# Convolution taps as one chain per channel group, the second half's first groups during the first attention, and squares summed on GpSimd

## The chip, the core and the metric

The kernel runs on one core of a Trainium2 chip. The metric is device time in microseconds (us) of one execution, lower is better; the kernel before takes 1140.39 us, the median of 3 runs. A core has five engines with their own instruction queues: TensorE (PE, matrix products), VectorE (DVE), ScalarE (ACT), GpSimd (POOL) and SyncE (SP, which only issues transfers here). Each engine works through its own queue strictly in order and waits for semaphores of the others. Products land in PSUM, which has eight banks of 128 x 512 float32; GpSimd does not touch PSUM in this kernel. Everything else lies in SBUF.

## The reference

One decoder layer over 1024 tokens of 1024 channels, in float32: an input projection, whose columns feed windowed attention (8 heads of 64, 2 key heads, window 128) and a convolution group (512 channels, 31 taps), both RMS-normalised and projected together, then a gated feed-forward layer with a 3-tap convolution. Both sub-layers end in a LayerNorm of the scaled input plus their output.

```python
def conformer_conv_group(a, gate, dw_w, dw_b, ln_g, ln_b):
    h = a * jax.nn.sigmoid(gate)
    h = causal_depthwise_conv(h, dw_w, dw_b)        # 31 taps, per channel
    h = layer_norm(h, ln_g, ln_b)                   # over the 512 channels
    return jax.nn.silu(h)

# sliding_window_gqa: each block of 128 queries sees its own and the previous key block
scores = jnp.where(mask, scores + bias[:, :, None], -jnp.inf)
m = jnp.maximum(jnp.max(scores, axis=-1, keepdims=True), sink)
p = jnp.exp(scores - m)
denom = jnp.sum(p, axis=-1, keepdims=True) + jnp.exp(sink - m)
probs = (p / denom).astype(v.dtype)

# hybrid_mixer
q, k, v, a, gate = jnp.split(x @ w_in + b_in, [Q_END, K_END, V_END, A_END], axis=-1)
y = jnp.concatenate([rms_norm(y_attn, attn_out_gain), rms_norm(y_conv, conv_out_gain)], axis=-1)
mix = y @ w_out + b_out
x = layer_norm(DEEPNORM_ALPHA * x + mix, ln1_g, ln1_b)

# conv_ffn
h = causal_depthwise_conv(x @ w_up, dw_w, dw_b)     # 3 taps
g, u = jnp.split(h, 2, axis=-1)
ffn = (jax.nn.silu(g) * u) @ w_down
x = layer_norm(DEEPNORM_ALPHA * x + ffn, ln2_g, ln2_b)
```

## The kernel before

The tokens are worked in two halves of 512 (`H` = 0 and 1), each as four tiles of 128. Channels lie on the 128 partitions, so one channel group is a tile of 128 x 512, and the convolution has four groups per half. For accuracy each float32 operand of a large product is split into a high and a low part (`wh`, `wl`; line 231 on ACT, line 233 on POOL), and three products replace one (`mm3`, lines 265, 266, 268).

Each step of a half is a Python generator: loading x (`x`), the gated input of the convolution (`0` for the first half, `g` for the second; `glu`), key and value (`j`, `k`), queries (`i`, `q`), convolution (`c`, `C`), its norm (`n`, `N`), attention (`a`, `A`), output projection (`o`, `O`), first LayerNorm (`l`, `L`) and the first six column pairs of the feed-forward layer for the first half (`f`). The string `SCRIPT` sets the program order: each letter runs its generator by one step, and `c` and `C` run to their end at once. From that program order a scheduler, with its own estimate of durations, sets the final order on every engine when the kernel is built. After the script the other sixteen column pairs are worked for both halves together (`joint`), then the rest of the second half.

**The convolution** (`conv_pair`, lines 405 to 430). The taps of one channel group are summed in one PSUM bank: line 421 starts the sum on DVE, and each further tap, line 425, reads the bank, adds one shifted, scaled copy of the input `hconv`, and writes it back. The oldest `KOFF` taps (4 in the first half, 5 in the second) are scaled on ACT (line 411) and summed on POOL (line 415), and line 430 adds the two sums. Two groups are worked together, tap by tap in turn, in the two banks tagged `C`. A dependency keeps all taps in one order.

**Its norm** (`conv_norm`, lines 441 to 485) sums the four groups over the channels: POOL adds (443, 444), one product with ones (445), DVE subtracts the mean (449), ACT squares (451), and sixteen products of one column (456, four token tiles by four groups) give the variance. Lines 462 and 464 spread the inverse deviation over the partitions, 469 to 472 apply it with swish and gain, 475 squares again, and sixteen more products (480) give the mean square for the RMS norm.

**The attention** (`attn`) has sixteen units per half: four token tiles, two key heads, two pairs of query heads. A unit's front makes scores (511), adds the bias and takes the row extreme on DVE (516), and the exponential on ACT (521) with the sink's exponential per head (523). After the second unit of a key head the denominator is made on DVE (527, 528) and ACT scales the four probability tiles (531). One unit later the tiles are transposed on PE (541) and split (543 on ACT, 544 on DVE), and one unit after that they are multiplied with the values (562 to 564). At the end of a token tile the result is scaled and split (569, 571), squared (574), and after three more units summed by four products of one column (581).

The output projection of a half (642 to 648, added up in 652 and 654) needs the whole norm of the convolution and the attention of the token tile. Line 627 prepares its accumulators. Other lines named below: 278, 281 and 282 transpose and split; 311 to 313 are the LayerNorm; 677 to 698 and 724 the first half's feed-forward work; 751 sums that prepare the joint stage; 806 and 808 its three-tap convolution.

## Time and profile before

| | |
|---|---|
| median of 3 runs | 1140.39 us (1139.77 to 1141.25) |
| the profiled execution | 1140.95 us, of which the profiled span is 1139.2 us |
| mean granted TensorE clock | 0.967 |
| PE busy | 1084.8 us (95%) |
| DVE busy | 776.6 us (68%) |
| POOL busy | 599.1 us (53%) |
| ACT busy | 521.3 us (46%) |
| HBM traffic | 84 MB, 74 GB/s |

The engines' shares are means over stages with different limits, so the stages are read one by one, in windows of the trace. The table of windows has, for each stretch of the span, the busy microseconds of each engine with its instruction count, then the granted clock and the share of the transfer engines. A matmul's record counts as busy also while the clock is lowered, so a busy PE may still be a slow one. A row of a group gives line, engine, operation, tiles and shape, then busy time, the mean duration of one, and the idle time ahead of them with what ended it.

### The profile page before, as it was taken

How to read it: one execution, taken by the hardware profiler on the slowest of the kernel's cores; microseconds unless marked ns; L12 is line 12 of the kernel's file. 1: busy time of each engine (PE TensorE's matmuls, PEld its weight loads, DVE VectorE, ACT ScalarE, POOL GpSimd, SP SyncE). 2: the span in 40 equal slices, each digit the busy share in tenths (PEclk: the TensorE clock that was granted, in tenths of full speed). 3: DMA queues.
4: the chain of work that ended last, by engine and by line, in shares of the span. 5: the costliest groups of instructions: out<-in, count | busy, mean ns of one | idle time of the engine just before them, and what ended most of it. 6: DMA issues, size and time to landing. Idle time of an engine off the chain costs nothing.

```text
span 1139.2 us, 14637 instructions
## 1 busy us (share of the span) xinstructions
PE 1084.8 (95%) x5257; PEld 903.9 (79%) x5257; DVE 776.6 (68%) x1414; ACT 521.3 (46%) x1031; POOL 599.1 (53%) x468
## 2 busy tenths in 40 slices
PE   7999999998888999989999999999999999999997
PEld 5877788888876899867778787878878787888875
DVE  3699555999996355998565747474656656559656
ACT  4536897673659432444424334251524242442530
POOL 4739645446461165834837465564636373835561
PEclk9999988999968899999999999999999999999998
DMA  5534212233220034113211112121212021223421
GB/s 179 167 97 116 72 32 66 83 93 119 67 93 19 1 121 120 57 38 92 73 38 56 56 38 75 37 75 37 65 28 75 19 75 37 70 99 115 125 93 74
DMA packets 115642, 85.21 MB, mean 75 GB/s; under 512 B 20354, under 2 KB 108017, under 8 KB 115569
## 3 DMA queue, kind: packets, MB, share of 16 engines
q1 hardware_dynamic: 112368, 78.92, 23.2%
q10 hardware_dynamic: 3201, 5.35, 1.3%
q8 instruction: 41, 0.67, 0.2%
q14 instruction: 32, 0.26, 0.1%
HBM read 80.05 MB, written 4.21 MB: 74 GB/s over the span
## 4 chain that ended last, share of the span: by engine, by line
PE 45%; DVE 5%; ACT 1%; DMA 0%; POOL 0%; issue 0%; POOLq 0%; ACTq 0%
PE psC L800 2%; PE psC L798 2%; PE psC L797 2%; PE psS L800 2%; PE psS L797 2%; PE psS L798 2%; PE psA L800 2%; PE psA L798 2%; PE psA L797 2%; PE psS L717 2%; PE psS L718 2%; PE psS L719 2%; PE psA L717 1%; PE psC L717 1%; PE psA L718 1%; PE psA L719 1%
## 5 line engine op out<-in xcount | busy, mean ns | idle before, releaser
L233 POOL TENSOR_TENSOR wl<-raw,wh 128x512 fp32r<-128x512 f32 x196 | 263.0, 1354 | 223.4 <-PE psA L268 86.3
L231 ACT CAST wh<-raw 128x512 fp32r<-128x512 f32 x196 | 118.7, 619 | 172.0 <-PE psA L266 19.2
L233 POOL TENSOR_TENSOR wl<-ts,wh 128x512 fp32r<-128x512 f32 x64 | 82.5, 1296 | 149.6 <-ACT wh L231 136.5
L265 PE MATMUL psA<-x,wh 128*128 128x512 f32 x336 | 138.2, 411 | 7.9 <-DVE z L682 3.5
L266 PE MATMUL psA<-x,wh 128*128 128x512 f32 x336 | 137.4, 409 | 0.0
L425 DVE SCALAR_TENSOR_TENSOR psC<-hconv,const,psC 128x512 f32<-128x512 f32 x196 | 135.8, 742 | 0.0
L231 ACT CAST wh<-ts 128x512 fp32r<-128x512 f32 x64 | 39.4, 622 | 174.4 <-PE psS L719 31.0
L268 PE MATMUL psA<-x,wl 128*128 128x512 f32 x336 | 90.6, 404 | 0.6 <-POOL wl L233 0.6
L265 PEld LDWEIGHTS psA<-x,wh 128*128 128x128 f32 x336 | 66.1, 197 | 24.0 <-issue 4.4
L266 PEld LDWEIGHTS psA<-x,wh 128*128 128x128 f32 x336 | 66.0, 197 | 14.6 <-issue 0.7
L268 PEld LDWEIGHTS psA<-x,wl 128*128 128x128 f32 x336 | 63.9, 193 | 15.8 <-issue 1.2
L293 POOL TENSOR_TENSOR tiny<-tiny,const 128x1 f32<-128x1 f32 (+1 forms) x28 | 27.6, 989 | 61.3 <-DVE tiny L292 61.3
L233 POOL TENSOR_TENSOR ol<-or,oh 128x512 fp32r<-128x512 f32 x32 | 41.0, 1307 | 26.8 <-PE psY L564 15.4
L724 DVE TENSOR_TENSOR acc<-psS,acc 128x512 f32<-128x512 f32 x52 | 35.6, 687 | 26.9 <-PE psS L719 26.9
L797 PE MATMUL psS<-x,wh 128*128 128x512 f32 x112 | 43.6, 389 | 0.0
L797 PE MATMUL psA<-x,wh 128*128 128x512 f32 x112 | 43.6, 389 | 0.0
L798 PE MATMUL psA<-x,wh 128*128 128x512 f32 x112 | 43.6, 389 | 0.0
L798 PE MATMUL psS<-x,wh 128*128 128x512 f32 x112 | 43.6, 389 | 0.0
L797 PE MATMUL psC<-x,wh 128*128 128x512 f32 x112 | 43.6, 389 | 0.0
L798 PE MATMUL psC<-x,wh 128*128 128x512 f32 x112 | 43.6, 389 | 0.0
L415 POOL TENSOR_TENSOR cp<-cp,cp 128x512 f32<-128x512 f32 x28 | 36.0, 1286 | 13.0 <-ACT cp L411 13.0
L836 POOL TENSOR_TENSOR ts<-raw,ts 128x512 f32<-128x512 f32 x32 | 41.6, 1299 | 1.2
(340 smaller groups left out, 3084.3 us busy)
## 6 DMA issues: line engine op xcount, KB each, us to landing
raw<-in_w_up SPq DMA_DIRECT2D x56, 512.0 KB
raw<-in_w_down SPq DMA_DIRECT2D x28, 512.0 KB
raw<-in_w_in SPq DMA_DIRECT2D x20, 512.0 KB
raw<-in_x SPq DMA_DIRECT2D x8, 512.0 KB
raw<-in_w_in SPq DMA_DIRECT2D x16, 256.0 KB
acc<-in_x SPq DMA_DIRECT2D x8, 512.0 KB
or<-in_w_out SPq DMA_DIRECT2D x64, 64.0 KB
or<-in_w_out SPq DMA_DIRECT2D x8, 512.0 KB
```

The source lines that it names most:

```text
L231: nc.scalar.copy(out=h, in_=part)
L233: nc.gpsimd.tensor_tensor(out=l, in0=part, in1=f(h), op=ALU.subtract)
L265: m.append(nc.tensor.matmul(out=o, lhsT=wh[kt], rhs=xh[kt], start=kt == 0, stop=False))
L266: m.append(nc.tensor.matmul(out=o, lhsT=wh[kt], rhs=xl[kt], start=False, stop=False))
L268: m.append(nc.tensor.matmul(out=o, lhsT=wl[kt], rhs=xh[kt], start=False, stop=kt == KT - 1))
L415: nc.gpsimd.tensor_tensor(out=extra[c], in0=extra[c], in1=prod, op=ALU.add)
L425: tap(nc.vector.scalar_tensor_tensor(out=to, in0=src, scalar=cdw(k, c), in1=chains[c], op0=ALU.mult, op1=ALU.add))
L717: m.append(nc.tensor.matmul(out=o, lhsT=gh[:, tsl], rhs=wh, start=j == 0, stop=False))
L797: m.append(nc.tensor.matmul(out=o, lhsT=wh[k], rhs=xh[k], start=k == 0, stop=False))
L798: m.append(nc.tensor.matmul(out=o, lhsT=wh[k], rhs=xl[k], start=False, stop=False))
L800: m.append(nc.tensor.matmul(out=o, lhsT=wl[k], rhs=xh[k], start=False, stop=k == 3))
L836: nc.gpsimd.tensor_tensor(out=t, in0=x0, in1=x1, op=ALU.subtract)
```

## The change

One change with seven pieces:

- **Script.** The second half's gated inputs begin earlier (two `g` stand ahead of the first convolution). `C` becomes a step per channel group: two groups are started right behind the first half's norm, ahead of most of the first attention, the third and fourth between later attention steps. The later letters move with them.
- **Chains.** `conv_group` works one channel group at a time in one bank `C`; the other bank becomes `N`, for the norm.
- **Token sums.** Both sums of squares of the norm are first added over the four groups on POOL (three additions of 128 x 512, line 433 of the changed kernel), so that four products of one column (435) replace sixteen.
- **Attention squares.** Two POOL additions (572, of 256 and 128 columns) let one product (578) replace four per token tile.
- **Sink.** One DVE addition (514) and one exponential of four columns (521) per key head replace four exponentials of one column.
- **Scaling.** The probability tiles are scaled by the inverse denominator on POOL (526), no longer on ACT.
- **Banks.** The joint stage and the second LayerNorm's transposes name the bank `N` in their rotations.

```diff
-SCRIPT = ('0hx00j0hxixxiiiacaaaaaaaaaaaaannnaaagaggqqgaaaqkqoAAAoAAAAAo'
-          'ACAoAAllAANAAAANAlAlfNfAOOOfsOsssffLLLLffff')
+SCRIPT = ('0hx00j0hxixxiiiggacaaaaaaaaaaaaannnCCaaagagCkCqqaaaqqoAAAoA'
+          'AAAAoAAoNAlAlNAlAlNAAAAfAfAAOOOfsOsssffLLLLffff')
...
-      'joint': 'ATSACSYC',
-      'tail': 'T', 'out0': 'A', 'out1': 'A', 'ln0': 'A', 'ln1': 'TC', 'sum1': 'T', 'up0': 'A', 'up1': 'AY', 'down0': 'SY', 'down1': 'S'}
-PS = {'A': 2, 'S': 2, 'T': 1, 'Y': 1, 'C': 2}
+      'joint': 'ATSACSYN',
+      'tail': 'T', 'out0': 'A', 'out1': 'A', 'ln0': 'A', 'ln1': 'TCN', 'sum1': 'T', 'up0': 'A', 'up1': 'AY', 'down0': 'SY', 'down1': 'S'}
+PS = {'A': 2, 'S': 2, 'T': 1, 'Y': 1, 'C': 1, 'N': 1}
...
-    def conv_pair(H, c0, dst):
...
-        chains = {c: psB(tag="C") for c in (c0, c0 + 1)}
         for k in range(KW - 1, KO - 1, -1):
-            for c in (c0, c0 + 1):
...
+    def conv_group(H, c, dst):
         KO = KOFF[H]
+        for k in range(KO):
+            slot = 2 * (c % 2) if k == 0 else 1
+            prod = at(64 * 4 * UNIT + 4 * (HC + slot * HALF), [P, HALF], F32, "cp")
+            nc.scalar.mul(out=prod, in_=hconv[H, c][:, k:k + HALF], mul=cdw(k, c))
+            if k == 0:
+                extra = prod
+            else:
+                nc.gpsimd.tensor_tensor(out=extra, in0=extra, in1=prod, op=ALU.add)
+        total = psB(tag="C")
+        for k in range(KW - 1, KO - 1, -1):
+            src = hconv[H, c][:, k:k + HALF]
+            if k == KW - 1:
+                tap(nc.vector.tensor_scalar(out=total, in0=src, scalar1=cdw(k, c), scalar2=cdb[c],
+                                            op0=ALU.mult, op1=ALU.add))
+            else:
+                tap(nc.vector.scalar_tensor_tensor(out=dst if k == KO else total, in0=src, scalar=cdw(k, c),
+                                                   in1=total, op0=ALU.mult, op1=ALU.add))
+        nc.gpsimd.tensor_tensor(out=dst, in0=dst, in1=extra, op=ALU.add)
...
+    def token_sums(o, sqs):
+        for a, b in ((0, 1), (2, 3), (0, 2)):
+            nc.gpsimd.tensor_tensor(out=sqs[a], in0=sqs[a], in1=sqs[b], op=ALU.add)
+        for t in range(TB):
+            nc.tensor.matmul(out=o[:, t:t + 1], lhsT=sqs[0][:, t * P:(t + 1) * P], rhs=ones[:, 0:1],
+                             start=True, stop=True)
...
-        for t in range(TB):
-            for c in range(4):
-                nc.tensor.matmul(out=var[:, t:t + 1], lhsT=sqs[c][:, t * P:(t + 1) * P], rhs=ones[:, 0:1],
-                                 start=c == 0, stop=c == 3)
+        token_sums(var, sqs)
...
+            if pr == 1:
+                nc.vector.tensor_tensor(out=es, in0=sink[:, g * 4:g * 4 + 4], in1=m, op=ALU.add)
             for i in range(2):
...
-                nc.scalar.activation(out=es[:, j:j + 1], in_=sink[:, h:h + 1], func=AF.Exp, bias=m[:, j:j + 1],
-                                     scale=1.0)
             pts[u] = pt
             if pr == 1:
+                nc.scalar.activation(out=es, in_=es, func=AF.Exp)
                 nc.vector.tensor_tensor(out=den, in0=den, in1=es, op=ALU.add)
                 nc.vector.reciprocal(out=den, in_=den)
                 for j in range(4):
                     q = pts[t, g, j // 2][:, j % 2, lo:]
-                    nc.scalar.mul(out=q, in_=q, mul=den[:, j:j + 1])
+                    nc.gpsimd.tensor_scalar(out=q, in0=q, scalar1=den[:, j:j + 1], scalar2=1.0,
+                                            op0=ALU.mult, op1=ALU.mult)
...
                 nc.scalar.square(out=sq, in_=yp[t])
+                for w in (2 * P, P):
+                    nc.gpsimd.tensor_tensor(out=sq[:, 0:w], in0=sq[:, 0:w], in1=sq[:, w:2 * w], op=ALU.add)
...
-            for i in range(4):
-                nc.tensor.matmul(out=ms[:, 0:1], lhsT=sqs[t][:, i * P:(i + 1) * P], rhs=ones[:, 0:1],
-                                 start=i == 0, stop=i == 3)
+            nc.tensor.matmul(out=ms[:, 0:1], lhsT=sqs[t][:, 0:P], rhs=ones[:, 0:1], start=True, stop=True)
...
     for k in SCRIPT:
-        if k in 'cC':
+        if k == 'c':
             drain(steps[k])
```

Three places of the new order follow. The first is DVE at the start of the first half's convolution (`hconv_30_238` is its input, `psC_...` a bank). Before:

```order
L358 SCALAR_TENSOR_TENSOR hconv_30_238<-psA_287,const_1_61,z_43_342 128x512
L421 TENSOR_SCALAR psC_799<-hconv_30_238,const_1_61 128x512
L425 SCALAR_TENSOR_TENSOR psC_798<-hconv_30_238,const_1_61,psC_798 128x512
L357 COPY hconv_71_1553<-hconv_30_238 128x30
L425 SCALAR_TENSOR_TENSOR psC_799<-hconv_30_238,const_1_61,psC_799 128x512
L425 SCALAR_TENSOR_TENSOR psC_798<-hconv_30_238,const_1_61,psC_798 128x512
L425 SCALAR_TENSOR_TENSOR psC_799<-hconv_30_238,const_1_61,psC_799 128x512
```

And in the changed kernel:

```order
L418 TENSOR_SCALAR psC_915<-hconv_30_238,const_1_61 128x512
L282 TENSOR_TENSOR x_39_263<-psS_272,x_38_262 128x4x128
L421 SCALAR_TENSOR_TENSOR psC_915<-hconv_30_238,const_1_61,psC_915 128x512 x12
L358 SCALAR_TENSOR_TENSOR hconv_30_238<-psA_287,const_1_61,z_43_342 128x512
L421 SCALAR_TENSOR_TENSOR psC_915<-hconv_30_238,const_1_61,psC_915 128x512
L357 COPY hconv_54_825<-hconv_30_238 128x30
L421 SCALAR_TENSOR_TENSOR psC_915<-hconv_30_238,const_1_61,psC_915 128x512 x11
```

Two banks that took turns have become one bank, where each tap reads what the tap just ahead of it wrote; the first chain starts with one gated group in place of two. The second place is DVE in the first attention, from the last tap of the first half on (`cy` is a finished convolution, `hank` the probability tiles, `ph` their transposes, `hconv_1553` or `hconv_825` the second half's input). Before:

```order
L425 SCALAR_TENSOR_TENSOR cy_780<-hconv_238,const_61,psC 128x512
L544 TENSOR_TENSOR ph_948<-psT,ph_948 128x256
L516 ISA hank_256,tiny_60<-psS,bias_573,const_61 128x256
L516 ISA tiny_60 128x1
...
L358 SCALAR_TENSOR_TENSOR hconv_1553<-psA,const_61,z_407 128x512
L544 TENSOR_TENSOR ph_967<-psT,ph_967 128x256
L527 TENSOR_TENSOR tiny_60<-tiny_60 128x4
L528 RECIPROCAL tiny_60<-tiny_60 128x4
```

And now:

```order
L418 TENSOR_SCALAR psC<-hconv_825,const_61 128x512
L540 TENSOR_TENSOR ph_1090<-psT,ph_1090 128x256
L510 ISA hank_256,tiny_60<-psS,bias_573,const_61 128x256
L510 ISA tiny_60 128x1
...
L421 SCALAR_TENSOR_TENSOR psC<-hconv_825,const_61,psC 128x512
L514 TENSOR_TENSOR tiny_60<-const_61,tiny_60 128x4
L421 SCALAR_TENSOR_TENSOR psC<-hconv_825,const_61,psC 128x512
L522 TENSOR_TENSOR tiny_60<-tiny_60 128x4
L421 SCALAR_TENSOR_TENSOR psC<-hconv_825,const_61,psC 128x512
L523 RECIPROCAL tiny_60<-tiny_60 128x4
```

Taps of the second half stand between the first attention's rows, and mostly alternate with them. The third place is POOL in the first attention, around the last additions of the first half's channel sum (`wl` is the low part of a weight tile, `cp` and `nsum` belong to the convolution, `nsq` are squares, `sq` the attention's). Before:

```order
L444 TENSOR_TENSOR nsum_1330<-nsum_1330,nsum_1331 128x512
L233 TENSOR_TENSOR wl_174<-raw_166,wh_284 128x512
L415 TENSOR_TENSOR cp_781<-cp_781,cp_783 128x512
L233 TENSOR_TENSOR wl_205<-raw_201,wh_168 128x512
L415 TENSOR_TENSOR cp_781<-cp_781,cp_783 128x512
L415 TENSOR_TENSOR cp_790<-cp_790,cp_783 128x512
L233 TENSOR_TENSOR wl_209<-raw_201,wh_172 128x512
```

And now, a few rows behind that addition (its row is line 444 there too):

```order
L526 TENSOR_SCALAR hank_258<-hank_258,tiny_60 128x256 x2
L526 TENSOR_SCALAR hank_260<-hank_260,tiny_60 128x256 x2
L233 TENSOR_TENSOR wl_170<-raw_346,wh_207 128x512
L413 TENSOR_TENSOR cp_944<-cp_944,cp_908 128x512
L233 TENSOR_TENSOR wl_174<-raw_166,wh_280 128x512
L433 TENSOR_TENSOR nsq_1451<-nsq_1451,nsq_1454 128x512
L433 TENSOR_TENSOR nsq_1457<-nsq_1457,nsq_1460 128x512
L413 TENSOR_TENSOR cp_944<-cp_944,cp_908 128x512
L233 TENSOR_TENSOR wl_205<-raw_166,wh_284 128x512
L433 TENSOR_TENSOR nsq_1451<-nsq_1451,nsq_1457 128x512
L233 TENSOR_TENSOR wl_209<-raw_201,wh_168 128x512
L572 TENSOR_TENSOR sq_1182<-sq_1182 128x256
```

Before, this queue held only the weight splits and the convolution's own additions there; the scalings 526 stood on ACT (531), and 433 and 572 did not exist.

More of the change, by code (lines that the diff above doesn't have):

```diff
@@ L432, in conv @@
-    def conv(H):
-        y = [sbt([P, HALF], "cy") for c in range(4)]
-        for c0 in (0, 2):
-            yield from conv_pair(H, c0, y)
-        cyt[H] = y
+        for k in range(KO):
[6 more added lines that the diff above has]
+                nc.gpsimd.tensor_tensor(out=extra, in0=extra, in1=prod, op=ALU.add)
@@ new lines, in conv_group @@
+        nc.gpsimd.tensor_tensor(out=dst, in0=dst, in1=extra, op=ALU.add)
+    def conv(H):
+        cyt[H] = [sbt([P, HALF], "cy") for c in range(4)]
+        for c in range(4):
+            conv_group(H, c, cyt[H][c])
+            yield
+    def token_sums(o, sqs):
[4 more added lines that the diff above has]
+                             start=True, stop=True)
@@ L476, in conv_norm @@
             sqs.append(sq)
-        ms = psB((P, 4), "C")
-        for t in range(TB):
-            for c in range(4):
-                nc.tensor.matmul(out=ms[:, t:t + 1], lhsT=sqs[c][:, t * P:(t + 1) * P], rhs=ones[:, 0:1],
-                                 start=c == 0, stop=c == 3)
+        ms = psB((P, 4), "N")
+        token_sums(ms, sqs)
         s = ring("sC", 4, 2)
```

28 lines of the change are left out of this document (3 added, 25 removed).

## The prediction

> **What bounds the kernel now.** I read the granted clock and span first, then the span in windows, then the waits in the windows that are not dense. The span and the windows, whose cuts are the last convolution tap of each half (128, 313), the second half's output projection (398 to 460) and the start of the joint stage (526):
>
> ```profile
> span 1139.2 us, 14637 instructions
> ...
> core 0: us, PE busy (x) PEld busy (x) DVE busy (x) ACT busy (x) POOL busy (x), PEclk, DMA share, GB/s
> 28.00:128.00 100.00, 98.91 (x448) 77.86 (x447) 85.75 (x159) 58.90 (x126) 63.99 (x51) 1.00 0.44 118
> 128.00:200.00 72.00, 72.00 (x352) 58.78 (x351) 34.06 (x88) 59.18 (x136) 38.63 (x34) 0.88 0.22 56
> 200.00:313.00 113.00, 106.10 (x710) 95.51 (x708) 109.93 (x233) 65.86 (x174) 56.42 (x45) 0.97 0.28 90
> 313.00:398.00 85.00, 73.64 (x349) 62.21 (x349) 55.41 (x117) 54.81 (x125) 26.18 (x18) 0.78 0.11 38
> 398.00:460.00 62.00, 61.86 (x463) 59.19 (x464) 35.89 (x71) 17.09 (x32) 37.10 (x29) 1.00 0.38 111
> 460.00:526.00 66.00, 61.31 (x274) 49.33 (x273) 59.50 (x89) 32.35 (x54) 39.56 (x27) 0.97 0.24 73
> 526.00:1139.00 613.00, 590.76 (x2585) 485.01 (x2583) 388.03 (x640) 220.80 (x372) 324.94 (x252) 0.99 0.20 64
> ```
>
> From 526 on PE is dense at full clock, and the change puts nothing there. Between 128 and 200, the first attention, DVE works 34 of 72 us while ACT works 59 of 72 and PE runs at a clock of 0.88. Between 200 and 313 it is the reverse: DVE is full (109.93 of 113) and PE waits 7 us. Between 313 and 398 no engine is full and the clock falls to 0.78. What DVE waits for in the first attention (two rows), and the waits of the stretch from 313 on (three):
>
> ```profile
> DVE hank L516 <- PE psT L541: 12.1, 6, 5.3
> DVE tiny L527 <- ACT tiny L523: 6.9, 4, 2.6
> ...
> POOL wl L233 <- PE psA L268: 27.7, 2, 24.7
> DVE ph L544 <- ACT ph L543: 12.2, 4, 6.6
> ACT ph L543 <- PE psT L541: 11.5, 3, 6.7
> ```
>
> So attention in both places is a chain over PE, ACT and DVE. Behind the last tap two chains run to the second output projection: the norm of the convolution and the last attention units.
>
> ```profile
> 312.34 0.73 DVE L425 SCALAR_TENSOR_TENSOR cy<-hconv,const,psC 128x512 f32<-128x512 f32 x1
> 326.65 2.47 DVE L449 TENSOR_TENSOR cy<-cy,psC 128x512 f32<-128x512 f32 x4
> ...
> L472 DVE SCALAR_TENSOR_TENSOR x<-cy,const,x x8: 751/752/796, 171.7 to 365.3; 128x512 fp32r<-128x512 f32 x8
> ...
> 398.42 0.39 PE L642 MATMUL psA<-oh,x 128*128 128x256 f32 x1
> ```
>
> The norm is done at 366, 53 us behind the last tap; the projection's first product starts at 398, behind the attention.
>
> **The change, part by part.** *Taps in one chain.* The spacing of taps that take turns in two banks, and of two DVE operations of the same width where the second reads what the first wrote:
>
> ```profile
> 59.49 9.30 DVE L425 SCALAR_TENSOR_TENSOR psC<-hconv,const,psC 128x512 f32<-128x512 f32 x14
> ...
> 554.71 0.75 DVE L806 SCALAR_TENSOR_TENSOR z<-psA,const,z 128x511 f32<-128x511 f32 x1 [0.85 <-ACT z L805]
> 555.49 0.75 DVE L808 SCALAR_TENSOR_TENSOR z<-psA,const,z 128x510 f32<-128x510 f32 x1
> ```
>
> Fourteen taps take 9.30 us, 0.66 from start to start ((9.30 - 0.74)/13); the dependent pair is 0.78 apart. So a tap right behind the tap that it depends on costs 0.12 more. Counted in the new order, 78 of the first half's 108 taps stand so, and 22 of the second half's 104. The first half pays 78 x 0.12 = 9.4 us of DVE between 28 and 128, where DVE has 14 us free and may start the chain earlier; I take 3 us on the path (0 to 10). The second half's 2.6 us go into the next term. The Trainium skill (VectorE: DVE Perf Modes, section The DRAIN you can't avoid) says that the next operation waits for an empty pipeline anyway and that a semaphore between two costs nothing extra. By that this term would be nothing and the sum 3 us lower; the two spacings above disagree.
>
> *Fewer one-column products.* The groups, a burst of them, and full products 0.43 apart behind it against 0.23 a little later:
>
> ```profile
> L456 PE MATMUL psC<-const,nsq 128*128 128x1 f32 x64 | 12.7, 322 | 2.5 <-ACT nsq L451 2.5
> L480 PE MATMUL psC<-const,nsq 128*128 128x1 f32 x64 | 9.4, 262 | 0.2 <-ACT cy L470 0.2
> L581 PE MATMUL psT<-const,sq 128*128 128x1 f32 x64 | 8.8, 258 | 0.0
> ...
> 152.50 4.55 PE L456 MATMUL psC<-const,nsq 128*128 128x1 f32 x26
> ...
> 160.64 0.63 PE L265 MATMUL psA<-x,wh 128*128 128x512 f32 x1
> 161.07 0.63 PE L266 MATMUL psA<-x,wh 128*128 128x512 f32 x1
> ...
> 164.42 0.39 PE L265 MATMUL psA<-x,wh 128*128 128x512 f32 x1
> 164.65 0.39 PE L266 MATMUL psA<-x,wh 128*128 128x512 f32 x1
> ```
>
> Three quarters of 192 passes go. At 0.175 each (4.55/26) the norm of one half sheds 48 x 0.175 = 8.4 us of PE; the tails shed 24 per half, at 8.8/64 = 0.14 some 3 us. In exchange POOL adds three tiles per sum.
>
> *ACT sheds, POOL takes.* What ACT loses and what POOL pays for work of nearby kinds:
>
> ```profile
> L531 ACT ACTIVATE hank<-hank,tiny 128x256 f32<-128x256 f32 x56 | 24.0, 502 | 3.2 <-DVE tiny L528 3.2
> L523 ACT ACTIVATE tiny<-const,tiny 128x1 f32<-128x1 f32 x64 | 18.1, 282 | 0.0
> ...
> L415 POOL TENSOR_TENSOR cp<-cp,cp 128x512 f32<-128x512 f32 x28 | 36.0, 1286 | 13.0 <-ACT cp L411 13.0
> L312 POOL TENSOR_TENSOR acc<-acc,g 128x1024 f32<-128x1024 f32 x8 | 19.8, 2482 | 6.0 <-DVE tiny L292 3.0 <-DVE acc L311 3.0
> L381 POOL MEMSET vpad<- 128x512 f32 x8 | 3.8, 526 | 0.3 <-POOLq L1057 0.3
> L293 POOL TENSOR_TENSOR tiny<-tiny,const 128x1 f32<-128x1 f32 x24 | 22.7, 947 | 55.0 <-DVE tiny L292 55.0
> L233 POOL TENSOR_TENSOR wl<-raw,wh 128x512 fp32r<-128x512 f32 x196 | 263.0, 1354 | 223.4 <-PE psA L268 86.3 <-ACT wh L231 68.5 <-PE psS L718 14.2
> ```
>
> ACT sheds 24 us of scaling and 18.1 - 16 x 0.28 = 13.6 us of sinks. A POOL addition of 256 columns is 0.69 by the line through 512 and 1024 columns (1.29 and 2.48). The scaling on POOL is in no row: half a fill bounds it below (0.26), the power on one column above (0.95); with one input it lies nearer the addition than the fill, and I take 0.5. Until the last tap POOL then gains some 48 wide and 8 narrow scalings (26 us), six token additions (6 x 1.29 = 8) and the attention squares (6): 40 us on 38.63 + 56.42 = 95. That fits into 185 us, so I cost it at nothing; without that cover it is the slower rival below.
>
> *Between 128 and 313.* Ahead of the end of the first half's norm stand 43 second-half taps in the new order, 1 in the old. DVE's work there is 34.06 + 109.93 = 144 us. To it come the 2.6 us, some ten new small additions (line 514) at 0.49, and some 3 us because operations with two SBUF inputs meet a busier POOL, as this one does:
>
> ```profile
> L527 DVE TENSOR_TENSOR tiny<-tiny x16: 143/424/1218, 117.8 to 369.8; 128x4 f32<-128x4 f32 x16
> ```
>
> (the mean, 7.8 us over 16, is 0.49; the least 0.14). That makes 155. PE's need, its busy time by its clock, is 72.00 x 0.88 + 106.10 x 0.97 = 166, less 11 of one-column passes: 155 too. With 97% density, as DVE has from 200 on, the stretch is 160 us; at today's 78% it would be 199. Two engines that need 155 each and wait for each other, with ACT no longer full: I take 90%, 172 us, a gain of 13 (25 to 0).
>
> *Between 313 and 398.* The move empties little of it: behind the last tap 12 score operations are left, before 14, and the same 96 weight products. PE sheds 8.4 + 1.4 us and ACT some 14 x (0.28 + 0.43) = 10 us. The end lies between 85 - 10 = 75 us and the norm's 54. The same chain over lines 541, 543 and 544 stays, so I take the upper part, 70: a gain of 15 (10 to 31).
>
> *The rest.* From 398 to 460 PE is full at clock 1.00 and unchanged. From 460 to 526 DVE has 59.5 of 66 us; the third bank can give 0 to 5, I take 1. In the joint stage each bank still serves once in eight.
>
> The sum against the profiled execution: 1140.95 + 3 - 13 - 15 - 1 = 1114.95. That execution is 0.56 us above the median 1140.39, so the median becomes 1114.4.
>
> **Rivals.** *Slower: scalings stuck in POOL's queue.* POOL is in order, and its weight splits wait for PE to free a buffer (86.3 us in all; one single wait of 24.7 us from 313 on). A scaling behind such a split holds up the transposes, and PE behind them, while PE's next weight product would have freed the buffer. One weight product is 24 x 0.228 = 5.5 us; if each of the sixteen groups of scalings loses half of one, the kernel gains 16 x 2.7 = 44 us over the forecast: 1158. It decides from 1.6 us per group on (26/16). At 0.95 per scaling POOL would be 94% busy until the last tap (95 + 66 of 172). Against it: a unit lies between scaling and transposes, and POOL rows with slack are what the new order shows.
>
> *Little gain: only PE's passes come off.* If attention stays the path and DVE gets no denser, 128 to 313 gives the 11 us of passes at most and 313 to 398 little: about 1130. The Trainium skill (SBUF — State Buffer, the section on the ports) says that GpSimd and a DVE operation with two SBUF inputs exclude each other for a whole instruction. The row of line 527 agrees in kind; by it 32 such additions, each at the row's longest wait, 1.2 in place of 0.49, cost 23 us, two thirds of it before the last tap, and the time would be 1130 as well.
>
> *Large gain: the clock comes back.* If the one-column bursts and the idle spells are what lowers the clock, both stretches near their bounds: 162 and 61 us, gains of 23 and 24, and 1094 to 1096.
>
> *No change* would need the gain of two stretches to cancel; that the taps do not move is excluded by the order.
>
> **How the numbers follow.** Forecast (1105 to 1125) 0.42; large gain 0.20; little gain 0.20; stuck scalings 0.14; no change 0.04. A move under 0.2%, 2.3 us, cannot be told from none for this kernel. So faster 0.82, same 0.04, slower 0.14. The range, 1094 to 1141, leaves out the slower case and the lower end of the large gain; the forecast's own is 1105 to 1125.
>
> **What would show it.** Right: dependent taps 0.78 apart; the last tap of the second half near 303 (128 + 3 + 172), the projection's first product near 373, and all later stretches as long as now. POOL between 128 and the last tap about 79% busy, with scalings near 0.5 us. Wrong: PE waiting for transposes of scaled tiles behind POOL, DVE still under 85% before the last tap, or a projection that starts no earlier relative to the last tap.

## The result, and the profile after

The changed kernel takes 1110.6 us, the median of 4 runs (1109.27 to 1113.39), against 1140.82 for the kernel before beside it: ratio 0.975, 95% interval 0.9726 to 0.9774. The forecast was 1114.4. Its profiled execution took 1113.39 us (span 1111.6), 27.56 us less than that of before; all comparisons of stretches below are between profiled executions.

The table of windows of the changed kernel, cut at its own marks: the end of the first half's last tap (135.2), of the second half's last tap (295.6), and the start of the second half's output projection (371.7). Columns as in the prediction's table.

```profile
135.20:295.60 160.40, 147.87 (x914) 126.52 (x915) 145.79 (x331) 98.59 (x236) 116.17 (x129) 0.99 0.29 83
295.60:371.70 76.10, 63.81 (x347) 54.05 (x346) 61.13 (x130) 43.10 (x94) 53.77 (x51) 0.84 0.15 49
371.70:1111.60 739.90, 711.85 (x3299) 591.73 (x3297) 480.58 (x793) 267.68 (x451) 398.06 (x303) 0.99 0.22 68
```

And the kernel before, at the same marks:

```profile
127.70:313.10 185.40, 178.40 (x1060) 154.51 (x1058) 144.39 (x323) 125.45 (x310) 95.35 (x79) 0.94 0.26 77
313.10:398.40 85.30, 73.92 (x349) 62.29 (x349) 55.71 (x117) 55.07 (x124) 26.58 (x18) 0.78 0.11 38
398.40:1139.20 740.80, 713.66 (x3317) 593.46 (x3317) 483.03 (x797) 269.88 (x456) 401.20 (x306) 0.99 0.22 69
```

The first half's last tap ends 7.5 us later, the stretch between the two last taps is 25.0 us shorter, the stretch to the projection 9.2, and from the projection on nothing moves (740.8 and 739.9). So the whole gain is made before the second output projection starts. Between the last taps DVE did the same work (144.39 and 145.79 us) in less time, 91% of it instead of 78; ACT shed 27 us, POOL took 21 more, and the clock rose from 0.94 to 0.99.

The marks themselves, rows of the changed kernel's timeline (start and length in us):

```profile
134.54 0.74 DVE L421 SCALAR_TENSOR_TENSOR cy<-hconv,const,psC 128x512 f32<-128x512 f32 x1
...
294.92 0.74 DVE L421 SCALAR_TENSOR_TENSOR cy<-hconv,const,psC 128x512 f32<-128x512 f32 x1
...
371.68 0.28 PE L638 MATMUL psA<-oh,x 128*128 128x256 f32 x1
```

### The profile page after: what moved, and what is told of

Same layout as the page of the kernel before. It is cut to its first block, busy times and chain, and to the rows that moved or that the text cites. A ratio compares the mean times of both kernels' runs of the same rounds, so it can differ in the third digit from the quotient of the medians.

```text
span 1111.6 us, 14383 instructions
## 1 busy us (share of the span) xinstructions
PE 1050.4 (94%) x5113; PEld 873.9 (79%) x5113; DVE 788.9 (71%) x1430; ACT 481.9 (43%) x915; POOL 654.5 (59%) x560
## 4 chain that ended last, share of the span: by engine, by line
PE 76%; DVE 13%; DMA 4%; POOL 3%; ACT 3%; issue 1%; SPq 0%; POOLq 0%; DVEq 0%; ACTq 0%
PE psA L265 6%; PE psA L266 6%; PE psA L268 5%; PE psS L713 2%; PE psS L714 2%; PE psS L715 2%; PE psS L796 2%; PE psS L794 2%; PE psS L793 2%; PE psA L794 2%; PE psA L796 2%; PE psA L793 2%; PE psS L505 2%; PE psA L638 1%; PE psA L713 1%
## 5 line engine op out<-in xcount | busy, mean ns | idle before, releaser
L421 DVE SCALAR_TENSOR_TENSOR psC<-hconv,const,psC 128x512 f32<-128x512 f32 x196 | 147.3, 751 | 3.5
L265 PE MATMUL psA<-x,wh 128*128 128x512 f32 x336 | 135.9, 404 | 7.9 <-DVE z L678 4.1
L266 PE MATMUL psA<-x,wh 128*128 128x512 f32 x336 | 134.4, 400 | 0.0
L268 PE MATMUL psA<-x,wl 128*128 128x512 f32 x336 | 87.2, 396 | 0.6 <-POOL wl L233 0.6
L265 PEld LDWEIGHTS psA<-x,wh 128*128 128x128 f32 x336 | 64.9, 193 | 23.9 <-issue 4.7
L266 PEld LDWEIGHTS psA<-x,wh 128*128 128x128 f32 x336 | 64.9, 193 | 13.5 <-issue 0.2
L268 PEld LDWEIGHTS psA<-x,wl 128*128 128x128 f32 x336 | 62.3, 188 | 15.1 <-issue 1.2
L793 PE MATMUL psA<-x,wh 128*128 128x512 f32 x112 | 43.6, 389 | 0.0
L794 PE MATMUL psA<-x,wh 128*128 128x512 f32 x112 | 43.6, 389 | 0.0
L713 PE MATMUL psS<-wh,gh 128*128 128x512 f32 x88 | 35.0, 397 | 5.9 <-ACT gh L693 3.1
L638 PE MATMUL psA<-oh,x 128*128 128x256 f32 x128 | 37.9, 296 | 1.9 <-ACT z L399 1.5
```

The source lines that it names most:

```text
L265: m.append(nc.tensor.matmul(out=o, lhsT=wh[kt], rhs=xh[kt], start=kt == 0, stop=False))
L266: m.append(nc.tensor.matmul(out=o, lhsT=wh[kt], rhs=xl[kt], start=False, stop=False))
L268: m.append(nc.tensor.matmul(out=o, lhsT=wl[kt], rhs=xh[kt], start=False, stop=kt == KT - 1))
L421: tap(nc.vector.scalar_tensor_tensor(out=dst if k == KO else total, in0=src, scalar=cdw(k, c), in1=total, op0=ALU.mult, op1=ALU.add))
L638: m.append(nc.tensor.matmul(out=pa[:, 0, :], lhsT=yah[:, c, :], rhs=wa[0][c], start=c == 0, stop=False))
L713: m.append(nc.tensor.matmul(out=o, lhsT=gh[:, tsl], rhs=wh, start=j == 0, stop=False))
```

## The experiments

Twelve kernels. The comparison of each is its ratio to the kernel before, run beside it. Where two variants are compared, the difference of their medians is followed by that of their ratios, times 1140 us, in brackets; the two differ since not all ran on the same occasion. Since in every profiled execution the time from the second projection's start to the end is the same (739 to 743 us), two lengths describe a kernel: **part 1**, up to the first score product of the second attention, and **part 2**, from there to the projection's first product. The last two columns split the time from 28 us to that product by PE: its work, each product counted with the spacing that its shape has in the undisturbed stretches of the kernel before (0.226 us for 512 columns, 0.120 for 256, 0.108 for a transpose, 0.111 for one column), and the rest, lost in waits and in a lowered clock.

| kernel | ratio, 95% interval | median, us | part 1 | part 2 | PE work | PE lost |
|---|---|---|---|---|---|---|
| before | 1 | 1140.8 | 229.9 | 168.5 | 295.9 | 74.5 |
| changed | 0.975 (0.9726 to 0.9774) | 1110.6 | 216.6 | 155.1 | 284.5 | 59.0 |
| old script | 0.9932 (0.991 to 0.9955) | 1132.6 | 217.9 | 169.1 | 282.6 | 76.4 |
| order alone | 0.9889 (0.9863 to 0.9915) | 1128.2 | 233.6 | 152.7 | 297.3 | 61.0 |
| scalings on ACT | 0.9825 (0.9791 to 0.9859) | 1120.7 | 213.6 | 164.5 | 283.4 | 66.6 |
| one-column products | 0.9876 (0.9849 to 0.9903) | 1127.1 | 226.6 | 159.3 | 299.6 | 58.3 |
| those of the norm | 0.9828 (0.9787 to 0.9869) | 1121.0 | 224.2 | 154.8 | 293.2 | 57.8 |
| sink exponentials | 0.985 (0.9804 to 0.9896) | 1119.8 | 216.2 | 162.4 | 282.9 | 67.7 |
| scalings twice | 0.9929 (0.9901 to 0.9957) | 1129.1 | 218.8 | 166.0 | 282.9 | 74.0 |
| six taps per group off DVE | 0.9869 (0.9813 to 0.9925) | 1121.3 | 218.2 | 154.7 | 282.5 | 62.3 |
| first half in pairs | 0.9711 (0.9665 to 0.9756) | 1103.9 | 214.5 | 148.2 | 282.4 | 52.3 |
| pairs, sink folded | 0.9739 (0.9697 to 0.9781) | 1110.0 | 217.2 | 148.1 | 281.7 | 55.9 |
| pairs, scalings shared | 0.9744 (0.9705 to 0.9783) | 1111.0 | 217.1 | 152.9 | 283.9 | 58.1 |
| before, single chains | 0.999 (0.9967 to 1.0012) | 1136.5 | 230.6 | 163.3 | 297.7 | 68.2 |

### The old script in the changed kernel

```diff
-SCRIPT = ('0hx00j0hxixxiiiggacaaaaaaaaaaaaannnCCaaagagCkCqqaaaqqoAAAoA'
-          'AAAAoAAoNAlAlNAlAlNAAAAfAfAAOOOfsOsssffLLLLffff')
+SCRIPT = ('0hx00j0hxixxiiiacaaaaaaaaaaaaannnaaagaggqqgaaaqkqoAAAoAAAAAo'
+          'ACAoAAllAANAAAANAlAlfNfAOOOfsOsssffLLLLffff')
...
-        if k == 'c':
+        if k in 'cC':
```

> All six other pieces stay, only the old script is put back (the second half's convolution starts behind the first attention, and runs at once). Theory 1, that the earlier taps carry the gain because they fill DVE while PE and ACT work the first attention: most of the gain goes, 1128 to 1138 us; DVE busy in the first attention falls back to under 60%, and the last tap of the second half lies near 310. Theory 2, that the relief of PE and ACT (fewer one-column products, sinks, scalings) carries it and the order is a detail: 1108 to 1118 us.

### The order alone

The script, the chains and the banks of the changed kernel; the four reliefs (token sums, attention squares, sink, scalings) taken out. Two of the four edits are shown; that of the sink stands in a later section.

```diff
-        for a, b in ((0, 1), (2, 3), (0, 2)):
-            nc.gpsimd.tensor_tensor(out=sqs[a], in0=sqs[a], in1=sqs[b], op=ALU.add)
         for t in range(TB):
-            nc.tensor.matmul(out=o[:, t:t + 1], lhsT=sqs[0][:, t * P:(t + 1) * P], rhs=ones[:, 0:1], ...)
+            for c in range(4):
+                nc.tensor.matmul(out=o[:, t:t + 1], lhsT=sqs[c][:, t * P:(t + 1) * P], rhs=ones[:, 0:1],
+                                 start=c == 0, stop=c == 3)
...
-                    nc.gpsimd.tensor_scalar(out=q, in0=q, scalar1=den[:, j:j + 1], scalar2=1.0, ...)
+                    nc.scalar.mul(out=q, in_=q, mul=den[:, j:j + 1])
```

> The counterpart: new script, single chains and the two banks, but the four reliefs taken out (sixteen products of one column per sum, four per attention tail, four sink exponentials, scalings on ACT). Theory 1: 1116 to 1124 us, last tap of the second half below 303. Theory 2: 1128 to 1140 us, with PE and ACT at the pace of the kernel before. If both this and the kernel with the old script lose most of the gain, neither works without the other.

Of the 1140.7 us beside them, the old script leaves a gain of 8.2 us and the order alone one of 12.5; the changed kernel has 30.2. Each of the two fits another theory, so neither held as it stood. Both kernels keep the single chains and the two banks, which no kernel tests alone; on top of them, by medians, the reliefs bring a quarter of the gain, the script four tenths, and the rest needs both. The windows say why. Four tables of two windows each, part 1 from the first half's last tap on and then part 2: of the kernel before, of the old script, of the order alone and of the changed kernel.

```profile
127.00:229.90 102.90, 102.90 (x510) 84.58 (x509) 64.78 (x144) 79.66 (x185) 51.55 (x42) 0.92 0.22 63
229.90:398.40 168.50, 150.12 (x904) 132.79 (x903) 136.02 (x298) 101.55 (x251) 71.07 (x55) 0.87 0.21 66
```

```profile
140.00:218.00 78.00, 73.92 (x366) 58.97 (x364) 72.41 (x123) 53.06 (x109) 62.62 (x61) 1.00 0.23 69
218.00:387.00 169.00, 138.62 (x851) 122.63 (x852) 142.98 (x309) 81.57 (x198) 99.92 (x108) 0.86 0.21 66
```

```profile
135.60:233.60 98.00, 94.86 (x454) 77.42 (x452) 84.30 (x174) 72.97 (x174) 51.59 (x42) 0.88 0.20 55
233.60:386.30 152.70, 142.55 (x923) 128.95 (x923) 114.68 (x268) 99.08 (x253) 59.77 (x48) 0.89 0.23 73
```

```profile
134.50:216.60 82.10, 79.53 (x401) 62.86 (x400) 72.73 (x155) 57.62 (x123) 65.23 (x71) 1.00 0.25 71
216.60:371.70 155.10, 132.85 (x860) 118.02 (x861) 134.90 (x306) 84.69 (x209) 104.70 (x110) 0.91 0.24 72
```

In these two kernels "the order" is the script with the chains and the banks. The reliefs act on part 1: PE's clock there is 1.00 with them (old script, changed) and 0.92 or 0.88 without, and part 1 ends 12.0 us earlier in the kernel with the old script, while part 2 stays (+0.6). The order acts on part 2, 15.8 us shorter, while part 1 gets 3.7 us longer. Together they give 13.3 and 13.4: the order lengthens part 1 only where the reliefs are missing. PE's columns show the same split: the old script has 13 us less of PE's work and no less of its losses, the order alone 13.5 us less of losses and no less work.

One expectation of the old script missed, and it changes what "order" means. DVE did not fall below 60% in the first attention: it worked 72.41 of 78 us, since the second half's taps start early there too, in the bank that is free:

```profile
142.04 0.80 DVE L418 TENSOR_SCALAR psC<-hconv,const 128x512 f32<-128x512 f32 x1
```

In the kernel before, the first chain starts at 174.2 and the second at 191.1, when the norm gives the two banks back, and 70 of the second half's 104 taps (counted by their rows) fall into part 2; with the old script 61, in the changed kernel 53, in the order alone 37. With the old script the chain starts 2 us behind the first half's last tap, ahead of the norm's sums and so of their relief. So it is the bank of its own, together with single chains, that lets the scheduler pull the taps into the first attention. The script moves eight more taps ahead (61 to 53), and takes 14.0 us from part 2 that are not the taps' alone (8 taps are 6 us). Which of its later letters gives the rest was not separated.

### One-column products, all of them and those of the norm

```diff
-        for a, b in ((0, 1), (2, 3), (0, 2)):
-            nc.gpsimd.tensor_tensor(out=sqs[a], in0=sqs[a], in1=sqs[b], op=ALU.add)
         for t in range(TB):
-            nc.tensor.matmul(out=o[:, t:t + 1], lhsT=sqs[0][:, t * P:(t + 1) * P], rhs=ones[:, 0:1], ...)
+            for c in range(4):
+                nc.tensor.matmul(out=o[:, t:t + 1], lhsT=sqs[c][:, t * P:(t + 1) * P], rhs=ones[:, 0:1],
+                                 start=c == 0, stop=c == 3)
```

The first of the two kernels also has the attention tails with four products and without the GpSimd additions.

> The changed kernel with sixteen products of one column per token sum and four per attention tail again (the GpSimd additions go with them). PE gets back 144 of the 192 products, about 22 us of records. If PE bounds the stretch before the second half's last tap and the norm behind it: 1118 to 1126 us, with a lower granted clock behind the bursts. If they only fill PE's waits: 1109 to 1114.

> The changed kernel with the norm's sixteen products of one column per sum again (without the three GpSimd additions), the attention tails left at one product. 48 of the 72 products that came back per half are here, in four bursts of 32. If the cost is that of the products and of the lower clock behind such a burst: 1119 to 1124 us, with granted clock 0.7 to 0.9 in the 20 us around each burst and 1.00 between 130 and 200 elsewhere. If the four products of each attention tail cost as much as their number says, or more: 1112 to 1117.

Both cost about what was expected if PE sets the pace: 16.5 us (14.4) for all 144 products, 1 us above the expected range, and 10.4 (8.9) for the norm's 96, within it and nearly in proportion. PE's work rises by 15.1 and 8.7 us and its losses in sum do not change. The price has two parts, the products' own time and a lower clock behind them. In part 1 from 28 us on the clock falls from 1.00 to 0.97 in both kernels, which is some 6 us of 196; since the losses stay the same in sum, PE's waits must be shorter elsewhere by about as much, so the second part is seen in the clock and not in the total. The kernel with the norm's products, in windows of 10 us:

```profile
170.00:180.00 10.00, 10.00 (x41) 8.46 (x41) 7.51 (x17) 3.05 (x8) 4.93 (x7) 0.74 0.00 0
180.00:190.00 10.00, 10.00 (x50) 7.84 (x49) 8.03 (x16) 9.51 (x17) 7.32 (x7) 1.00 0.25 54
...
200.00:210.00 10.00, 10.00 (x45) 8.56 (x45) 9.93 (x16) 3.57 (x9) 10.00 (x12) 0.66 0.01 4
```

And rows of its timeline at the start of the last of these windows:

```profile
199.09 0.39 PE L265 MATMUL psA<-x,wh 128*128 128x512 f32 x1
199.31 0.39 PE L266 MATMUL psA<-x,wh 128*128 128x512 f32 x1
199.54 2.96 PE L434 MATMUL psN<-const,nsq 128*128 128x1 f32 x26
202.43 1.62 PE L504 MATMUL psS<-kh,x 64*128 64x256 f32 x6
203.98 0.79 PE L265 MATMUL psA<-x,wh 128*128 128x512 f32 x1
204.57 0.63 PE L266 MATMUL psA<-x,wh 128*128 128x512 f32 x1
204.99 0.63 PE L265 MATMUL psA<-x,wh 128*128 128x512 f32 x1
```

Twenty-six products of one column take 2.96 us (0.114 each); ahead of them full products stand 0.22 apart, behind them 0.42, and the clock of the window falls to 0.66. In the timeline of the changed kernel such a burst is eight products long (0.95 us), and full products behind it stand 0.23 apart:

```profile
174.92 0.95 PE L435 MATMUL psN<-const,nsq 128*128 128x1 f32 x8
175.73 0.49 PE L265 MATMUL psA<-x,wh 128*128 128x512 f32 x1
176.06 0.39 PE L266 MATMUL psA<-x,wh 128*128 128x512 f32 x1
176.29 0.40 PE L265 MATMUL psA<-x,wh 128*128 128x512 f32 x1
```

Such a burst does not always do this. In the kernel before with single chains, further below, the same twenty-six products take the same 2.96 us at 381 us, and the clock stays:

```profile
381.23 2.96 PE L481 MATMUL psC<-const,nsq 128*128 128x1 f32 x26
```

```profile
380.00:390.00 10.00, 10.00 (x66) 8.95 (x65) 3.83 (x8) 2.39 (x4) 1.03 (x1) 1.00 0.00 0
```

The Trainium skill (TensorE: Matmul & The Clock Gate, Part 1) says that the array falls to half its clock after an idle window of about 3.4 us. The trace agrees with the half (0.42 against 0.22); PE's row here shows no gap, so in this place a burst of one-column products had the effect that the Trainium skill gives to idleness.

### Scalings on ACT, and the sink's exponentials on ACT

```diff
-                    nc.gpsimd.tensor_scalar(out=q, in0=q, scalar1=den[:, j:j + 1], scalar2=1.0, ...)
+                    nc.scalar.mul(out=q, in_=q, mul=den[:, j:j + 1])
```

> The changed kernel with the scaling of the probability tiles on ACT again. If ACT is off the path once DVE is the fuller engine: 1109 to 1114 us. If ACT's 24 us of scalings lie on the chain from PE over ACT to DVE in attention: 1118 to 1128. If the scalings stuck behind weight splits on GpSimd cost something even now: under 1107.

```diff
-            if pr == 1:
-                nc.vector.tensor_tensor(out=es, in0=sink[:, g * 4:g * 4 + 4], in1=m, op=ALU.add)
...
+                nc.scalar.activation(out=es[:, j:j + 1], in_=sink[:, h:h + 1], func=AF.Exp, bias=m[:, j:j + 1], scale=1.0)
...
-                nc.scalar.activation(out=es, in_=es, func=AF.Exp)
```

> The changed kernel with four sink exponentials of one column per key head on ACT again, without the DVE addition. ACT gets 13.6 us back, about 7 of them in the second attention. If ACT's share of the attention chain sets the second attention's length, as the kernel with the scalings on ACT says (5 to 10 us for 24 us of ACT): 1113 to 1117 us. If not: 1109 to 1112.

They cost 10.1 us (8.6) and 9.2 (11.4), both in part 2 (+9.4 and +7.3), neither in part 1. The scalings cost what was expected if they lie on the attention chain; the sinks cost 2.8 us more than that range. Both speak for ACT's share of the chain setting the length of the second attention, even where ACT is busy only 85 of 155 us: it would then be the time of one unit's chain that counts, not the engine's load. That step is argued; no wait is shown for it, and the sinks' 7.3 us is as much as ACT's whole added work there (about 7). The costs of single undos must not be added, though: script, one-column products, scalings and sink come to 22.0 + 16.5 + 10.1 + 9.2 = 58 us, twice the whole gain, and the order alone, which undoes the last three together, is 17.6 us (15.8) slower than the changed kernel.

### Scalings twice

```diff
+                    nc.gpsimd.tensor_scalar(out=q, in0=q, scalar1=1.0, scalar2=1.0, op0=ALU.mult, op1=ALU.mult)
```

> The changed kernel with each scaling on GpSimd followed by a second one by 1.0, in place: 64 more operations of 0.47 us, 30 us more for GpSimd, 1.9 us behind each group of four. GpSimd then works about 140 of the 161 us between the two last taps. If scalings behind weight splits hold up the transposes (the slower rival of the prediction, deciding from 1.6 us per group on): 1120 to 1140 us. If GpSimd's slack still covers it: 1109 to 1114.

GpSimd's slack does not cover it: 18.5 us (20.4) more, in the range of the slower rival. PE loses 15 us more, most of it in part 2. But the mechanism is not the rival's. Two of the largest waits between 219 and 340 us in this kernel (us in total, times, longest):

```profile
ACT ph L540 <- PE psT L538: 25.2, 10, 5.2
ACT tiny L521 <- DVE tiny L514: 12.8, 6, 4.5
```

And its timeline, DVE and then GpSimd at the same time:

```profile
222.12 0.68 DVE L541 TENSOR_TENSOR ph<-psT,ph 128x512 fp32r<-128x512 f32 x1
222.72 5.43 DVE L514 TENSOR_TENSOR tiny<-const,tiny 128x4 f32<-128x4 f32 x1
228.08 1.53 DVE L421 SCALAR_TENSOR_TENSOR psC<-hconv,const,psC 128x512 f32<-128x512 f32 x2
...
222.78 0.40 POOL L528 TENSOR_SCALAR hank<-hank 128x256 f32<-128x256 f32 x1
223.15 1.29 POOL L423 TENSOR_TENSOR cy<-cy,cp 128x512 f32<-128x512 f32 x1
224.41 3.73 POOL L233 TENSOR_TENSOR ol<-or,oh 128x512 fp32r<-128x512 f32 x3
229.75 0.55 POOL L293 TENSOR_TENSOR tiny<-tiny,const 128x1 f32<-128x1 f32 x1 [1.62 <-DVE tiny L522]
```

No transpose in this kernel is shown waiting for a scaled tile. ACT's wait for transposes is large in the changed kernel too (21.6 us in its part 2). What is new is the wait of the sink's exponential (4.5 us there), for a DVE addition of four columns that here takes 5.43 us: it starts while GpSimd is busy and ends at 228.15, when GpSimd pauses. How much of the 18.5 us is due to such additions and how much to the longer scalings themselves was not separated.

### First half in pairs

```diff
+    def conv_pair(H, c0, dst):
...
+        chains = {c: psB(tag="CN"[c - c0]) for c in (c0, c0 + 1)}
...
+        if H == 0:
+            for c0 in (0, 2):
+                conv_pair(H, c0, cyt[H])
+            return
```

> The changed kernel, but the first half's channel groups are convolved two at a time again, in the banks C and N (N is free until the norm). The second half stays in single chains. By the prediction's term, dependent taps cost the first half about 3 us on the path (0 to 10): 1101 to 1108 us. Rival: PE was full at clock 1.00 between 28 us and the first half's last tap (107.04 of 107.2 us), so the later last tap is no loss there and PE's pace is all that counts: 1109 to 1113 us, with the first half's last tap near 128 all the same.

`conv_pair` works two groups tap by tap in turn, as before the change. It is the fastest kernel here, within the range that the prediction's term gave: 1103.9 us (1103.23 to 1105.8), 6.7 us (4.4) under the changed kernel, with no run of the one within the range of the other. The intervals of the two ratios overlap, though (0.9665 to 0.9756 and 0.9726 to 0.9774), since they come from different occasions. In its timeline taps stand 0.66 apart again:

```profile
44.83 0.75 DVE L446 SCALAR_TENSOR_TENSOR psC<-hconv,const,psC 128x512 f32<-128x512 f32 x1
45.49 0.75 DVE L446 SCALAR_TENSOR_TENSOR psN<-hconv,const,psN 128x512 f32<-128x512 f32 x1
46.15 0.75 DVE L446 SCALAR_TENSOR_TENSOR psC<-hconv,const,psC 128x512 f32<-128x512 f32 x1
```

The first half's last tap starts at 122.6 instead of 134.5, the second half's at 280.4 instead of 294.9, and part 2 is 6.9 us shorter.

### The kernel before with single chains in the first half

```diff
-        for k in range(KW - 1, KO - 1, -1):
-            for c in (c0, c0 + 1):
+        for k, c in ([(k, c) for c in (c0, c0 + 1) for k in range(KW - 1, KO - 1, -1)] if H == 0 else
+                     [(k, c) for k in range(KW - 1, KO - 1, -1) for c in (c0, c0 + 1)]):
+            if True:
```

> The kernel before, with one edit: in the first half the taps of a channel group stand in one chain behind each other, group after group, as in the changed kernel (banks, script and the second half's pairs as before). It pays the same dependent taps without anything that could repay them. The prediction's term, 3 us (0 to 10), gives 1143.5 us, ratio 1.0026. If the 6.7 us by which the changed kernel gains with pairs is the price of dependent taps on the path: 1146 to 1150 us, ratio 1.005 to 1.008. If that gain was only another order of the rest, or the earlier start of the first chain repays the taps: 1138 to 1142.5, ratio 0.998 to 1.002.

The taps pay their price, as a row of its timeline shows, twelve of them (9.45 - 0.75)/11 = 0.79 apart:

```profile
32.91 9.45 DVE L426 SCALAR_TENSOR_TENSOR psC<-hconv,const,psC 128x512 f32<-128x512 f32 x12
```

The first half's last tap starts at 140.2 instead of 127.0, the second half's at 320.5 instead of 312.3, and the time is the same: ratio 0.999 (0.9967 to 1.0012). So no cost of dependent taps is seen in the time of the kernel before. The likely reason is that DVE was idle for half of the stretch behind them (34.06 of 72 us busy in the prediction's table) and that the taps take from there. This is not shown beyond doubt: part 1 is 0.7 us longer and part 2 is 5.2 shorter, so another order of the rest may have paid for a cost of up to some 5 us.

### One more tap per group off DVE, and two variants of the pairs

```diff
-KOFF = (4, 5)
+KOFF = (4, 6)
```

> The changed kernel with six instead of five of the second half's oldest taps on ACT and GpSimd: DVE loses four taps (3.1 us), ACT gains 4 x 0.6 us and GpSimd 4 x 1.29 us. If DVE sets the stretch between the two last taps: 1107 to 1109 us. If PE's work and its waits for the attention chain set it: 1109 to 1113 us, though the last tap comes 3 us earlier.

The last tap comes 10 us earlier (284.7), yet the projection starts 1.2 us later in the profiled execution (1114.0), and the median is 10.7 us (13.6) above the changed kernel's. Both ranges, 1107 to 1113 together, missed: there is no gain. The runs of this kernel lie far apart (1114.0 to 1124.2), so more than that is not to be read from it.

```diff
-        nc.vector.tensor_scalar(out=nsink, in0=sink, scalar1=-1.0, scalar2=None, op0=ALU.mult)
+        nc.vector.memset(nsink, 0.0)
+        nc.vector.tensor_tensor(out=tab[0:NBUCKET, :], in0=tab[0:NBUCKET, :], in1=sink[0:NBUCKET, :], op=ALU.subtract)
...
-                nc.vector.tensor_tensor(out=es, in0=sink[:, g * 4:g * 4 + 4], in1=m, op=ALU.add)
...
-                nc.scalar.activation(out=es, in_=es, func=AF.Exp)
+                nc.scalar.activation(out=es, in_=m, func=AF.Exp)
```

> The kernel with the first half in pairs, and the sink folded into the bias table (once, 32 x 8 values), so that the row extreme is already relative to the sink and the DVE addition of four columns (line 514 of the changed kernel) goes. Those sixteen additions took 0.15 to 2.5 us each there, and the sink exponential waited 9.3 us for them. If a DVE operation with two SBUF inputs that is held up by GpSimd lies on the attention chain: 1092 to 1100 us, against 1103.9 with the additions. If the chain had slack there: 1102 to 1106.

```diff
-                    nc.gpsimd.tensor_scalar(out=q, in0=q, scalar1=den[:, j:j + 1], scalar2=1.0, ...)
+                    if j < 2:
+                        nc.scalar.mul(out=q, in_=q, mul=den[:, j:j + 1])
+                    else:
+                        nc.gpsimd.tensor_scalar(out=q, in0=q, scalar1=den[:, j:j + 1], scalar2=1.0, ...)
```

> The kernel with the first half in pairs, and the four scalings of a key head shared: two on ACT, two on GpSimd. GpSimd loses 15 us, ACT gains 12. The doubled scalings cost 18 us, so a group's 1.9 us on GpSimd is on the attention chain; two and two take about 1 us instead. If that latency counts: 1094 to 1101 us. If two engines to wait for are no better than one: 1102 to 1110.

Both missed: 1110.0 and 1111.0, above even the ranges for no gain (to 1106 and to 1110), and both a little slower than the pairs without them (ratios 0.9739 and 0.9744 against 0.9711, intervals overlapping). Taking sixteen additions away leaves part 2 as it was (148.1 and 148.2), so in the pairs kernel nothing shows them on the path, whatever they cost in the kernel with scalings twice. These misses also set a limit to the reading. Parts 1 and 2 come from one profiled execution of each kernel; each variant is put in order anew by the scheduler, and part 2 of the kernel before with single chains became 5.2 us shorter although nothing of it was edited. A difference of some 5 us between two variants need not come from the edit.

## Why the prediction was right

The forecast, 1114.4 in 1105 to 1125, held with 1110.6. In its own steps, on profiled executions: foreseen were +3 - 13 - 15 - 1 = -26 us, measured -27.56. The direction, the places of the gain and the price of a tap were foreseen; that the sum came so close is luck in part, since the terms were off in ways that offset each other (7.5 for 3, 25.0 for 13, 9.2 for 15).

**+3, dependent taps.** The price per tap was right: the rows of the changed kernel stand 0.79 apart (0.78 foreseen), 78 in the first half and 22 in the second, as counted. What it costs on the path was mis-sized, and not in one direction. The last tap came 7.5 us later, but PE had by then done 484 products since 28 us, the kernel before 446 by its own mark; so the mark moved, and work moved ahead of it. The windows up to that mark, of the changed kernel and of before:

```profile
28.00:135.20 107.20, 107.04 (x484) 85.31 (x483) 94.16 (x157) 60.90 (x117) 75.57 (x63) 1.00 0.44 118
```

```profile
28.00:127.70 99.70, 98.61 (x446) 77.64 (x445) 85.45 (x159) 58.59 (x124) 63.69 (x51) 1.00 0.44 118
```

In the old order no price on the path is seen (0.999). In the new order the pairs gain 6.7 us (4.4), more than the 3. The likely reason, argued rather than shown, is that the new order leaves DVE no idle time behind the first half to absorb it: 62.16 of 72 us are busy there now, as this window of the changed kernel shows, and further on about nine tenths.

```profile
128.00:200.00 72.00, 71.13 (x352) 55.95 (x352) 62.16 (x143) 54.12 (x118) 56.85 (x62) 1.00 0.22 55
```

That one more tap per group off DVE gained nothing speaks against so simple a reading, so the share of another order in the 6.7 us stays open.

**-13, between the last taps.** It was 25.0 us. The density chosen, 90%, was right (145.79 of 160.4 us, 91%). What failed is the sum of DVE's and PE's needs, 155 each: some 9 us of both had moved ahead of the first mark. Taken without that mark, from 28 us to the second half's last tap, -17.5 us stand against the foreseen -10. The price of a one-column product was too high as well: 0.175 us, from a burst behind which the clock was low, where the burst of twenty-six above has 0.114. The clock probably explains a part that the prediction gave to the rival of the large gain: 1.00 from 128 to 200 us instead of 0.88.

**-15, behind the last tap.** It was 9.2 us, 76.1 left instead of 70, at the end that the prediction had called its bound (75). PE still stands at a clock of 0.84 and is busy 64 of 76 us, and the norm is late: its subtraction starts 23.2 us behind the last tap, before 14.3 (312.34 to 326.65). One wait there, of 4.3 us, is PE's for GpSimd's channel sum. That this lateness is what is missing is not shown: the norm's last DVE row ends at 356.0, 15.7 us ahead of the projection, and from 345 us on PE is full at clock 1.00. PE's time is lost before that, between 305 and 345 us, where it is busy 27.7 of 40 us at clocks of 0.50 to 0.84. The subtraction in the timeline of the changed kernel, the wait, and two of its windows:

```profile
318.10 1.87 DVE L449 TENSOR_TENSOR cy<-cy,psN 128x512 f32<-128x512 f32 x3
```

```profile
PE psN L445 <- POOL nsum L444: 4.3, 1, 4.3
...
335.00:345.00 10.00, 6.92 (x35) 5.81 (x34) 10.00 (x20) 7.16 (x17) 8.61 (x10) 0.66 0.00 0
345.00:355.00 10.00, 10.00 (x53) 8.52 (x53) 5.57 (x9) 9.97 (x16) 3.92 (x3) 1.00 0.01 2
```

**-1, the rest.** It was -0.9 (740.8 to 739.9).

**What was costed at nothing.** POOL's additions and scalings: 0.476 us for a scaling (0.5 foreseen), POOL busy 116 of 160 us, 72% (79% foreseen). They are hidden, but not with much to spare: the kernel with scalings twice lost 18.5 us.

**The rivals.** *Stuck scalings* did not come: transposes and their weight loads, counted together, waited 5.7 us for scalings in the whole kernel. Where the scalings were doubled (1.9 us more per group) the time rose by 18.5 us, but by other waits than the rival named. The scalings' line, and from the transposes' line what they waited for:

```profile
L526 POOL TENSOR_SCALAR hank<-hank,tiny x64: 364/476/906, 125.6 to 341.9; 128x256 f32<-128x256 f32 x56, 128x128 f32<-128x128 f32 x8
```

```profile
  POOL hank L526: 5.7, 4
```

*Little gain, PE's passes alone* fell by the order alone, which has none of the passes taken off and still wins 12.5 us, and by the old script, which has them off and wins 8.2, where 11 were allowed it. Its second form, additions held up by GpSimd, did not come either: the 32 additions of lines 514 and 522 take 12.4 us in the changed kernel, 0.39 each, not 1.2. *Large gain, the clock comes back* was half right: the clock came back in the first attention, where the bursts had been, and not behind the second half's last tap (0.84), where PE waits; its 1094 to 1096 needed both.

## What to carry to other kernels

Where one stage leaves DVE idle and the next is full of it, look first at what keeps the work from moving: here it was a bank shared with the norm. What a slower form of an instruction costs probably depends on the idle time behind it (dependent taps showed no cost where DVE waited anyway). Many products of one column cost PE their own time and often the clock behind them, so that adding the tiles on an engine with slack first pays. Do not share a gain out by undoing one piece at a time: the single undos here add up to twice the gain, and a variant that is put in order anew can move by some 5 us by itself.

## What the runs showed of the hardware

**A DVE addition can be held up over several GpSimd instructions.** The addition of 128 x 4 values takes 0.13 us at best and took 5.43 where, behind the GpSimd instruction that it met, one of 0.40 and four of about 1.3 us followed each other. All sixteen in the kernel with scalings twice (least, median and longest in ns):

```profile
L514 DVE TENSOR_TENSOR tiny<-const,tiny x16: 129/434/5433, 118.5 to 352.3; 128x4 f32<-128x4 f32 x16
```

The Trainium skill (SBUF — State Buffer, the section on the ports) says that a GpSimd instruction and a DVE operation with two SBUF inputs lock each other out for a whole instruction. The trace agrees in kind. In three of the sixteen (5.43, 4.78 and 4.77 us) DVE did not even get its turn between two GpSimd instructions, but only when GpSimd's row ended. That is not the rule: most of the others that met GpSimd ended with the one instruction that they met, though the next followed at once, and in the changed kernel none of the sixteen takes longer than 1.215 us. What decides between the two was not found. The taps from the second on, which read one of their operands from a bank, are not held up: in the whole changed kernel none takes longer than 0.757 us.

```profile
L421 DVE SCALAR_TENSOR_TENSOR psC<-hconv,const,psC x196: 721/756/757, 33.6 to 293.2; 128x512 f32<-128x512 f32 x196
```

**A dense row of one-column products often lowers PE's clock**, as shown above: 26 in 2.96 us, then half speed in one kernel and no change in another; eight in 0.95 us left the clock alone in the place shown. What decides was not found. PE counts as busy throughout, so the page's share of busy time shows nothing of it; only the granted clock and the spacing of the products behind do.
